# Spreading 1/rms with one-pass matmuls of a diagonal split in two, and another order of the last root

## The chip, the cores and the metric

The kernel runs on one core of a Trainium2 chip. A core has five engines with instruction queues of their own: PE (TensorE, matrix multiply), DVE (VectorE), ACT (ScalarE), POOL (GpSimd) and SP (SyncE, which issues DMAs here). Each works off its queue in order and waits for semaphores of the others. Times are microseconds on the device, from one launch of the whole layer; lower is better. The profile times every instruction of one execution.

## The reference

One decoder layer on x of 512 tokens by 1024 channels, all float32:

```
x = x + 0.5 * rms_norm(swiglu(rms_norm(x, g), w_gu, w_down), g')        # first network, d_ff = 2816
y = hybrid_mixer(rms_norm(x, g))          # RG-LRU channels beside sliding-window attention, then w_o
x = x + rms_norm(y, g')
x = x + 0.5 * rms_norm(swiglu(rms_norm(x, g), w_gu, w_down), g')        # second network
rms_norm(x, g) = x * rsqrt(mean(x * x, over channels) + 1e-6) * g
```

Each norm needs one factor 1/rms for every token. The mixer's recurrent half also has a norm of its own ahead of w_o.

## The kernel before, in words

**Layout.** Nearly everywhere activations lie with channels on the partitions and tokens along the free dimension: eight tiles of 128 channels by 512 tokens. Only the end of the second network has tokens on the partitions, four blocks of 128 tokens.

**Matmuls in three parts.** Weights and activations are split into a high part in the type float32r and a low part, the rest. A product is high x high, high x low and low x high, three matmuls of float32r operands (mm3, L502). The high part of a weight is made on ACT, the low part on DVE or POOL (L194 and L214 lie in these helpers; one weight is shared, half of its low part on DVE and half on POOL, class Shared). An activation's parts are made by x_high (ACT, L580) and x_low (DVE scalar_tensor_tensor, L583).

**From a sum of squares to a factor for each column.** Class InvRms does half of the tokens, 256. stats sums squares over the partitions with small matmuls, so that the sums of two token blocks stand in two columns with tokens on the partitions. invert makes the root on ACT (L556), the reciprocal on DVE (L558), and then a diagonal matrix of the factors on DVE (L560): the identity times the factors, two 128 x 128 blocks side by side, 256 columns. spread multiplies a matrix of ones with it (L564), which puts the factors of all 256 tokens on every partition; its result is read by DVE or copied by ACT. Both operands are float32, and the profile shows two LDWEIGHTS and two MATMUL records for each such matmul.

There are twelve spreads. Pair x is for the first norm (made in InvRmsX.early from sums of squares by token: for each half a sum L1179, the root, the reciprocal, the diagonal). Two single ones scale the first network's output in the first boundary, pair mx is for the mixer's input, pair lru for the recurrent half, two single ones stand in the second boundary, and pair f2 (named nf in the profile) is for the second network's input. A norm's factor is applied after the next products where that can be, so the pairs mx and f2 come in the middle of a stage.

**A boundary** (function boundary) ends one stage and begins the next. The last three output chunks are computed for the first half of the tokens, then for the second, with the first half's statistics and spread put into the second half's matmuls as hooks. Then DVE scales a chunk by the factor (L715), DVE or POOL adds it to the residual (L719), ACT makes its high part (L580) and PE multiplies it (L524, L525); low parts come later (L583 and L531).

**The order** of each engine's queue is the order of the program text. The weights' queue (class Weights) is filled some units ahead at places written by hand (W.fill).

**The end.** For each block of 128 tokens the second network's output is finished in two pieces, the last block in three (512, 256 and 256 columns). For each piece DVE adds the product's bank to a partial sum (L1983), ACT squares it with its sum into one column of the tile ss (L1984), and DVE or POOL multiplies the piece by the gain (L1988). Then DVE adds the columns (for the last block L1986 and L1990), ACT takes the root (L1995), DVE the reciprocal (L1996), and for each piece one instruction that scales and adds x (L1999), after which it is written out.

Of the kernel before, what the change touches and what calls it, by code (L numbers as in the profile page):

```python
# [8 lines left out]
F32 = mybir.dt.float32  # L9
F32R = mybir.dt.float32r  # L10
U8 = mybir.dt.uint8
AF = mybir.ActivationFunctionType
ALU = mybir.AluOpType
AX = mybir.AxisListType

P = 128
T = 512
NB = T // P
D = 1024
# [6 lines left out]
EPS = 1e-6  # L26
# [95 lines left out]
def tile_layer(ctx: ExitStack, tc: tile.TileContext, out: bass.AP, **ins: bass.AP):  # L122
    nc = tc.nc
    pe, dve, act, pool, sync = nc.tensor, nc.vector, nc.scalar, nc.gpsimd, nc.sync

    const = ctx.enter_context(tc.tile_pool(name="const", bufs=1))
# [3 lines left out]
    small = ctx.enter_context(tc.tile_pool(name="small", bufs=4))  # L130
# [6 lines left out]
    HALF = [slice(0, T // 2), slice(T // 2, T)]  # L137
# [6 lines left out]
    def t2k(name, dt=F32):  # L144
        return big.tile([P, T], dt, tag="t2k", name=name, bufs=NT2K)
# [16 lines left out]
    def wt(name, w=T, dt=F32):  # L162
        return tmp.tile([P, w], dt, tag="w", name=name, bufs=NW)
# [23 lines left out]
    class Shared:  # L187


        parts = slice(0, KD // 2), slice(KD // 2, KD)  # L190
# [273 lines left out]
    ident = const.tile([P, P], F32, name="ident")  # L464
# [3 lines left out]
    def filled(name, w, value):  # L468
        t = const.tile([P, w], F32, name=name)
        dve.memset(t, value)  # L470
        return t

    ones = filled("ones", P, 1.0)
    mean_d = filled("mean_d", 1, 1.0 / D)
    mean_c = filled("mean_c", 1, 1.0 / C)
    eps = filled("eps", 1, EPS)
    eps4 = filled("eps4", 1, 4 * EPS)
# [31 lines left out]
    def product(w, xs, sl=ALL, name="", hooks=()):  # L509
        ps = bank(name)  # L510
        hooks = dict(hooks)
        for k, x in enumerate(xs):
            if k in hooks:
                hooks[k]()
            mm3(ps[:, sl], w, k, [t[:, sl] for t in x], k == 0, k == len(xs) - 1)
        return ps
# [22 lines left out]
    class InvRms:  # L539
# [13 lines left out]
        def invert(self, ms, scale=1.0):  # L553
            n = self.name
            rms = small.tile([P, 2], F32, tag="rms", name=f"rms_s{n}")
            act.activation(rms, ms, AF.Sqrt, bias=self.eps, scale=scale)  # L556
            rs = small.tile([P, 2], F32, tag="rs", name=f"rs_{n}")
            dve.reciprocal(rs, rms)  # L558
            self.dg = wt(f"dg_{n}", T)[:, :2 * P].rearrange("p (a b) -> p a b", a=2)
            dve.tensor_tensor(self.dg, ident.unsqueeze(1).to_broadcast([P, 2, P]), rs.unsqueeze(2).to_broadcast([P, 2, P]), op=ALU.mult)  # L560

        def spread(self):
            o = self.ps[:, T // 2:]
            pe.matmul(o, ones, self.dg.rearrange("p a b -> p (a b)"), start=True, stop=True)  # L564
            return o


# [153 lines left out]
    def boundary(res, late, xs, parts, nxt, name):  # L721
# [21 lines left out]
        def spread_a():  # L743
            spread(0)
            steps((0, 1), 0, bcs[0])
# [35 lines left out]
        for k in range(KD):  # L781
            nxt.low(k, 0)
        k_high(ws, banks, nxt.xs, HALF[0], range(4, 6))
        spread(1)
        for k in range(0, KD, 2):
            steps((k, k + 1), 1, bcs[1])
# [571 lines left out]
    parts = [None] * KD  # L1358
    late, h_hbm, decay = [], {}, []
    for g, (f0, f1) in enumerate(GROUPS1):  # L1360
# [18 lines left out]
        for c in range(KD):  # L1379
# [25 lines left out]
            b = pair_banks[c] if c < 2 else product(W.take(), xs, name=f"ya{g}{c}")  # L1405
# [16 lines left out]
    def in_product(name, hooks=(), ahead=AHEAD):  # L1422
        return product(W.take(ahead), mx.xs, name=name, hooks=hooks)
# [79 lines left out]
    for j in range(4):  # L1503
        b = in_product(f"pq{j}")
# [90 lines left out]
    scale = HD ** -0.5  # L1595
# [215 lines left out]
    for c in range(EARLY):  # L1811
# [9 lines left out]
        if c == EARLY - 2:  # L1821
            bcs = [l.spread() for l in lrms]
            for ci in range(KC):
                for h in range(2):
                    dve.tensor_mul(hl[ci][:, HALF[h]], hl[ci][:, HALF[h]], bcs[h])
                y = t2k(f"ylh{ci}", F32R), t2k(f"yll{ci}", F32R)
# [39 lines left out]
    parts = {(tb, dh): hbm.tile([P, T], F32, name=f"yp_b{tb}{dh}") for tb in range(NB) for dh in range(2)}  # L1866
# [29 lines left out]
    def read(half, dh):  # L1896
        for tb in (2 * half, 2 * half + 1):
            in_hbm[tb, dh] = parts[tb, dh]
            parts[tb, dh] = t2k(f"yp{tb}{dh}")
            sync.dma_start(parts[tb, dh], in_hbm[tb, dh])  # L1900
# [3 lines left out]
    def read_x(i):  # L1904
        x = wpool.tile([P, 2 * D], F32, tag="raw", name=f"x_rows{i}", bufs=NRAW)
        for j in range(2):
            x_rows.append(x[:, j * D:(j + 1) * D])
            sync.dma_start(x_rows[-1], x_hbm[(2 * i + j) * P:(2 * i + j + 1) * P])

    grow = []  # L1910

    def read_gain():
        for dh in range(2):
            grow.append(t2k(f"grow{dh}"))
            sync.dma_start(grow[dh], ins["ffn2_post_g"][0:1, dh * T:(dh + 1) * T].to_broadcast([P, T]))

    last = {-1: [lambda: (read(0, 0), read(0, 1), read(1, 0), read(1, 1), read_gain(), read_x(0))],
            2: [lambda: hid.fetched(f0, h_hbm[f0])], 3: [lambda: read_x(1)], 4: [lambda: (hid.split(f0), hid.split(f0 + 1))]}
# [42 lines left out]
    pieces = {tb: [(0, 0, T)] + ([(1, 0, T // 2), (1, T // 2, T)] if tb == NB - 1 else [(1, 0, T)]) for tb in range(NB)}  # L1961

    def place(tb, i):
        dh, c0, c1 = pieces[tb][i]
        return kept[tb // 2, dh][tb % 2][:, c0:c1] if i < 2 else final[:, :c1 - c0]

    def out_products(tb, i, fs):
        dh, c0, c1 = pieces[tb][i]
        for f in fs:
            mm3_out(place(tb, i), hs[f - f0], tb, weights(f, dh), f % 2, slice(c0, c1), i == 2 and f == f0, f == f1 - 1, skip_group_check=True)  # L1970
# [4 lines left out]
    for tb in range(NB):  # L1975
        end = tb == NB - 1
        last = []
        ss = small.tile([P, 3], F32, tag="ss3", name=f"ss_b{tb}")
        tot = small.tile([P, 1], F32, tag="tot", name=f"tot_b{tb}")
        for i, (dh, c0, c1) in enumerate(pieces[tb]):  # L1980
            out_products(tb, i, range(f0 + 2 * ((tb, i) in started), f1))
            y = parts[tb, dh][:, c0:c1]
            dve.scalar_tensor_tensor(y, place(tb, i), -1.0 if dh else 1.0, y, op0=ALU.mult, op1=ALU.subtract if dh else ALU.add)  # L1983
            act.activation(wt(f"ysq{tb}{i}")[:, :c1 - c0], y, AF.Square, accum_out=ss[:, i:i + 1])  # L1984
            if end and i == 2:
                dve.tensor_add(tot, ss[:, 0:1], ss[:, 1:2])  # L1986
            last.append(wt(f"last{tb}{i}")[:, :c1 - c0])
            (dve if end or i else pool).tensor_mul(last[i], y, grow[dh][:, c0:c1])  # L1988
        if end:
            dve.tensor_add(tot, tot, ss[:, 2:3])  # L1990
        else:
            dve.tensor_add(tot, ss[:, 0:1], ss[:, 1:2])

        rs = small.tile([P, 1], F32, tag="rs1", name=f"rs_b{tb}")
        act.activation(rs, tot, AF.Sqrt, bias=eps4, scale=4.0 / D)  # L1995
        dve.reciprocal(rs, rs)  # L1996
        for i, (dh, c0, c1) in enumerate(pieces[tb]):
            y = parts[tb, dh][:, c0:c1]
            dve.scalar_tensor_tensor(y, last[i], rs, x_rows[tb][:, dh * T + c0:dh * T + c1], op0=ALU.mult, op1=ALU.add)  # L1999
            (act if end and i == 1 else sync).dma_start(out[0, tb * P:(tb + 1) * P, dh * T + c0:dh * T + c1], y)  # L2000
# [28 lines left out]
```

## Time and profile before

| what | before |
|---|---|
| median of three runs | 845.54 us (845.32 to 846.01) |
| span of the profiled execution | 843.6 us |
| PE busy | 834.5 us, 99% |
| DVE busy | 732.7 us, 87% |
| ACT busy | 523.8 us, 62% |
| POOL busy | 201.7 us, 24% |
| mean granted TensorE clock | 0.998 |

The span goes from the first to the last instruction of the profiled execution, which has no run time of its own beside it; what lies around it is 1.94 us if it ran like the median. In a row of the time order stand the start in the span, the duration, the engine, the line, the operation, "what is written <- what is read", the shape and the number of instructions that are merged in the row (x8); at the end, in brackets, how long the engine stood idle before it and who ended that. A duration runs from start to complete end, so the next instruction of an engine may start before it. In the chain of waits stand start, length, engine, tile and line.

### The profile page before, as it was taken

The numbers are of one execution on the slowest core, as the hardware profiler recorded it, in microseconds if no ns is written. First come the engines' busy times: TensorE is split into PE (matmuls) and PEld (weight loads), VectorE is DVE, ScalarE is ACT, GpSimd is POOL, SyncE is SP. The second block draws the span as 40 slices with busy tenths as digits, with TensorE's granted clock in tenths as the row PEclk, the third lists the DMA queues.
The fourth block names the chain that finished last, engine by engine and source line by source line (L and its number), as shares of the span: only waits on it lengthen the run. The fifth ranks groups of instructions, "written<-read, shape, count | busy, mean of one in ns | idle before, by whom it ended". The sixth has DMA issues, their size and how long they took to land.

```text
span 843.6 us, 12618 instructions
## 1 busy us (share of the span) xinstructions
PE 834.5 (99%) x4568; PEld 722.6 (86%) x4568; DVE 732.7 (87%) x1020; ACT 523.8 (62%) x874; POOL 201.7 (24%) x214
## 2 busy tenths in 40 slices
PE   9999999999999999999999999999999999999996
PEld 8988888988988998997788899888888888888885
DVE  4978999998979865889899589799998998998996
ACT  6646856666666655456788457436757767666552
POOL 2023000140320333334646055112004113032001
PEclk9999999999999999999999999999999999999999
DMA  7249419397595799222511131169539939769742
GB/s 251 77 131 348 151 59 322 80 254 254 129 248 185 169 261 343 77 79 91 158 50 51 50 110 42 50 137 273 186 108 231 322 91 249 249 154 262 295 137 101
DMA packets 123615, 143.75 MB, mean 170 GB/s; under 512 B 23896, under 2 KB 81568, under 8 KB 123040
## 3 DMA queue, kind: packets, MB, share of 16 engines
q1 hardware_dynamic: 109232, 111.86, 41.6%
q0 software_dynamic: 14176, 30.94, 17.0%
q8 instruction: 36, 0.59, 0.3%
q14 instruction: 27, 0.22, 0.1%
q10 hardware_dynamic: 144, 0.13, 0.0%
HBM read 100.45 MB, written 40.89 MB: 168 GB/s over the span
## 4 chain that ended last, share of the span: by engine, by line
PE 97%; ACT 1%; DVE 1%; DMA 1%; issue 0%; POOL 0%; DVEq 0%; POOLq 0%; ACTq 0%
PE ab L955 10%; PE aa L955 10%; PE da L955 5%; PE db L955 5%; PE yaa L1345 3%; PE bb L955 3%; PE ba L955 3%; PE yda L1345 2%; PE ya L507 2%; PE ya L505 2%; PE ya L506 2%; PE a_first L1205 1%; PE aa L885 1%; PE yab L1875 1%; PE yab L1874 1%; PE yab L1876 1%
## 5 line engine op out<-in xcount | busy, mean ns | idle before, releaser
L1115 POOL DMA_DIRECT2D yp_a<-stage x42 | 36.9, 1085 | 181.2 <-ACT stage L1112 160.9
L1115 POOL DMA_DIRECT2D yp_b<-stage x42 | 36.4, 1091 | 144.6 <-ACT stage L1112 121.1
L505 PE MATMUL ya<-hha,whi_ad 128*128 128x512 f32 x62 | 24.1, 389 | 0.0
L506 PE MATMUL ya<-hla,whi_ad 128*128 128x512 f32 x62 | 24.1, 389 | 0.0
L507 PE MATMUL ya<-hha,wlo_ad 128*128 128x512 f32 x62 | 24.1, 389 | 0.0
L688 POOL TENSOR_TENSOR acca_r<-acca_r,sq_r 128x512 f32<-128x512 f32 x6 | 8.2, 1359 | 51.4 <-ACT sq_r L536 51.4
L1988 POOL TENSOR_TENSOR last<-yp,grow 128x512 f32<-128x512 f32 x3 | 3.9, 1290 | 57.7 <-DVE yp L1983 57.7
L524 PE MATMUL an<-xh_mx,whi_xl 128*128 128x256 f32 x64 | 15.8, 287 | 0.0
L1984 ACT ACTIVATE ysq<-yp 128x512 f32<-128x512 f32 (+1 forms) x9 | 5.3, 585 | 16.5 <-DVE yp L1983 16.0
L525 PE MATMUL an<-xh_mx,wlo_xl 128*128 128x256 f32 x64 | 15.5, 283 | 0.0
L505 PE MATMUL gt<-xh_mx,whi_gt 128*128 128x512 f32 x32 | 14.2, 444 | 0.0
L1112 ACT COPY stage<-yab 128x512 f32<-128x512 f32 x12 | 6.5, 604 | 11.7 <-DMA yp_b<-stage 7.4
L507 PEld LDWEIGHTS ya<-hha,wlo_ad 128*128 128x128 f32 x62 | 11.6, 188 | 2.4
L506 PEld LDWEIGHTS ya<-hla,whi_ad 128*128 128x128 f32 x62 | 11.6, 188 | 2.4
L505 PEld LDWEIGHTS ya<-hha,whi_ad 128*128 128x128 f32 x62 | 11.6, 188 | 2.4
L536 ACT ACTIVATE sq_r<-yp_a 128x256 f32<-128x256 f32 (+1 forms) x10 | 5.0, 502 | 12.9 <-DVE yp_a L678 5.9
L505 PE MATMUL pq<-xh_mx,whi_q 128*128 128x512 f32 x32 | 12.8, 400 | 0.0
L505 PE MATMUL pub<-xh_f,whi_bu 128*128 128x512 f32 x32 | 12.6, 395 | 0.0
L507 PE MATMUL gt<-xh_mx,wlo_gt 128*128 128x512 f32 x32 | 12.6, 394 | 0.0
L505 PE MATMUL pgb<-xh_f,whi_bg 128*128 128x512 f32 x32 | 12.6, 393 | 0.0
L506 PE MATMUL gt<-xl_mx,whi_gt 128*128 128x512 f32 x32 | 12.5, 392 | 0.0
L580 ACT ACTIVATE xh_f<-xT,cols 128x256 fp32r<-128x256 f32 x16 | 8.1, 509 | 7.0 <-DVE xT L719 6.4
(2014 smaller groups left out, 3535.0 us busy)
## 6 DMA issues: line engine op xcount, KB each, us to landing
yp_a<-stage POOLq DMA_DIRECT2D x50, 256.0 KB, 8.9
yp_b<-stage POOLq DMA_DIRECT2D x50, 256.0 KB, 9.2
h_a<-za SPq DMA_DIRECT2D x16, 256.0 KB
hxa<-h_a SPq DMA_DIRECT2D x16, 256.0 KB
h_b<-zb SPq DMA_DIRECT2D x16, 256.0 KB
hxb<-h_b SPq DMA_DIRECT2D x16, 256.0 KB
xn<-in_x SPq DMA_DIRECT2D x8, 256.0 KB
xT_hbm<-xT POOLq DMA_DIRECT2D x2, 1024.0 KB, 9.7
```

Of the source, the lines that this page charges most:

```text
L505: pe.matmul(ps, hi[:, k, :], xh, start=start, stop=False)
L506: pe.matmul(ps, hi[:, k, :], xl, start=False, stop=False)
L507: pe.matmul(ps, lo[:, k, :], xh, start=False, stop=stop)
L524: pe.matmul(ps[:, sl], hi[:, k, :], xh, start=k == 0, stop=False)
L525: pe.matmul(ps[:, sl], lo[:, k, :], xh, start=False, stop=False)
L885: pe.matmul(o, w[:, k, js], x, start=first and i + j + k == 0, stop=k == 3 and i == 2, skip_group_check=True)
L955: pe.matmul(b[tb], x[:, blk], w[:, k, :], start=first and q + k + j == 0, stop=q + k == 2 and j == 2, skip_group_check=True)
L1115: pool.dma_start(o, st.rearrange("p (a b) -> p a b", a=2) if len(o.shape) == 3 else st, accum_op=ALU.add)
L1205: pe.matmul(banks[j][:, HALF[0]], ws[j][part][:, k, :], n1.xs[k][xpart][:, HALF[0]], start=k == 0 and part == xpart, stop=stop and k == KD ...
L1345: pe.matmul(o, a[:, k, ms], x[:, js], start=first and i + k + m % 2 == 0, stop=k == 1 and i == 2, skip_group_check=True)
L1874: pe.matmul(banks[i], hh[:, js], hi[:, k, :], start=first and k == 0, stop=False, skip_group_check=True)
L1875: pe.matmul(banks[i], hh[:, js], lo[:, k, :], start=False, stop=False, skip_group_check=True)
```

## The change

In InvRms the diagonal becomes two: a high part in float32r, written by the same tensor_tensor, and a low part, identity times factor minus the high part, written by two scalar_tensor_tensor of 128 columns, one for each token block. The matrix of ones becomes float32r (by a copy from a float32 one at the start), and spread becomes two matmuls of 256 columns, ones times the high and ones times the low part, summed in the same bank.

At the end, for the last block, the third sum of squares goes to a tile of its own. The other two are summed beside the last Square, already scaled by 4/D and with 4 eps added, and enter the root as its bias, so the root follows the last Square on ACT. The products with the gain of the second and third piece move behind the root in the program; the first stays.

```diff
-    ones = filled("ones", P, 1.0)
+    ones = const.tile([P, P], F32R, name="ones")
+    ones_f = wt("ones_f", P)
+    dve.memset(ones_f, 1.0)
+    dve.tensor_copy(ones, ones_f)
...
             dve.reciprocal(rs, rms)
-            self.dg = wt(f"dg_{n}", T)[:, :2 * P].rearrange("p (a b) -> p a b", a=2)
-            dve.tensor_tensor(self.dg, ident.unsqueeze(1).to_broadcast([P, 2, P]), rs.unsqueeze(2).to_broadcast([P, 2, P]), op=ALU.mult)
+            both = wt(f"dg_{n}", T, F32R)
+            self.dg = [both[:, sl] for sl in HALF]
+            hi, lo = (t.rearrange("p (a b) -> p a b", a=2) for t in self.dg)
+            dve.tensor_tensor(hi, ident.unsqueeze(1).to_broadcast([P, 2, P]), rs.unsqueeze(2).to_broadcast([P, 2, P]), op=ALU.mult)
+            for i in range(2):
+                dve.scalar_tensor_tensor(lo[:, i], ident, rs[:, i:i + 1], hi.bitcast(F32)[:, i], op0=ALU.mult, op1=ALU.subtract)
 
         def spread(self):
             o = self.ps[:, T // 2:]
-            pe.matmul(o, ones, self.dg.rearrange("p a b -> p (a b)"), start=True, stop=True)
+            for i, part in enumerate(self.dg):
+                pe.matmul(o, ones, part, start=i == 0, stop=i == 1)
             return o
...
-            act.activation(wt(f"ysq{tb}{i}")[:, :c1 - c0], y, AF.Square, accum_out=ss[:, i:i + 1])
-            if end and i == 2:
-                dve.tensor_add(tot, ss[:, 0:1], ss[:, 1:2])
+            if i == 2:
+                ss_last = small.tile([P, 1], F32, tag="tot", name="ss_last")
+                act.activation(wt(f"ysq{tb}{i}")[:, :c1 - c0], y, AF.Square, accum_out=ss_last)
+                dve.tensor_scalar(tot, ss[:, 0:1], 4.0 / D, 4 * EPS, op0=ALU.mult, op1=ALU.add)
+                dve.scalar_tensor_tensor(tot, ss[:, 1:2], 4.0 / D, tot, op0=ALU.mult, op1=ALU.add)
+            else:
+                act.activation(wt(f"ysq{tb}{i}")[:, :c1 - c0], y, AF.Square, accum_out=ss[:, i:i + 1])
             last.append(wt(f"last{tb}{i}")[:, :c1 - c0])
-            (dve if end or i else pool).tensor_mul(last[i], y, grow[dh][:, c0:c1])
+            if not end or i == 0:
+                (dve if end or i else pool).tensor_mul(last[i], y, grow[dh][:, c0:c1])
+        rs = small.tile([P, 1], F32, tag="rs1", name=f"rs_b{tb}")
         if end:
-            dve.tensor_add(tot, tot, ss[:, 2:3])
+            act.activation(rs, ss_last, AF.Sqrt, bias=tot, scale=4.0 / D)
+            for i, (dh, c0, c1) in list(enumerate(pieces[tb]))[1:]:
+                dve.tensor_mul(last[i], parts[tb, dh][:, c0:c1], grow[dh][:, c0:c1])
         else:
             dve.tensor_add(tot, ss[:, 0:1], ss[:, 1:2])
-
-        rs = small.tile([P, 1], F32, tag="rs1", name=f"rs_b{tb}")
-        act.activation(rs, tot, AF.Sqrt, bias=eps4, scale=4.0 / D)
+            act.activation(rs, tot, AF.Sqrt, bias=eps4, scale=4.0 / D)
         dve.reciprocal(rs, rs)
```

## The prediction, made before the change was run

> **What bounds the kernel.** I read the page's first part, then who waits for whom on PE, then the time order around each place that the change touches.
>
> ```profile
> span 843.6 us, 12618 instructions
> ...
> PE 834.5 (99%) x4568; PEld 722.6 (86%) x4568; DVE 732.7 (87%) x1020; ACT 523.8 (62%) x874; POOL 201.7 (24%) x214
> ```
>
> ```profile
> PE yeb L1876 <- DVE hls L838: 0.3, 1, 0.3
> ```
>
> PE works 834.5 of 843.6 us, and behind the start its longest wait is 0.3 us. So a microsecond taken off PE is a microsecond off the end, as long as DVE (87% busy) still delivers in time. Where PE is full, DVE has no slack to read from shares; it has to be read at each place.
>
> **Prices.** The chain of waits in time order at the first pair of spreads, a row of PE in time order, DVE rows, and a DVE row that met POOL:
>
> ```profile
> 28.70 0.86 PE rms_x L564 x4
> ```
>
> ```profile
> 354.76 4.00 PE L531 MATMUL an<-xl_mx,whi_xl 128*128 128x256 f32 x32
> ```
>
> ```profile
> 32.89 0.42 DVE L647 TENSOR_TENSOR tb_a<-xb_a,ta_a 128x256 f32<-128x256 f32 x1
> 33.34 0.43 DVE L648 TENSOR_TENSOR tb_a<-xb_a,tb_a 128x256 f32<-128x256 f32 x1
> ```
>
> ```profile
> 351.44 3.25 DVE L583 SCALAR_TENSOR_TENSOR xl_mx<-xT,cols,xh_mx 128x256 fp32r<-128x256 f32 x8
> 354.61 0.48 DVE L715 SCALAR_TENSOR_TENSOR yp_a<-yp_a,half_g,rms_r 128x256 f32<-128x256 f32 x1
> ```
>
> ```profile
> 472.07 0.75 DVE L583 SCALAR_TENSOR_TENSOR yll<-xc,cols,ylh 128x512 fp32r<-128x512 f32 x1 [0.79 <-ACT ylh L580]
> ```
>
> ```profile
> 391.57 1.32 POOL L1473 TENSOR_TENSOR xcl<-xc,xch 128x512 fp32r<-128x512 f32 x1 [1.05 <-ACT xch L1472]
> ```
>
> ```profile
> 391.67 1.77 DVE L1446 SCALAR_TENSOR_TENSOR xc<-xp,cols,xc 128x512 f32<-128x512 f32 x1
> ```
>
> PE: two spreads are four records, 0.86 us, 0.43 a spread. A one-pass matmul of 256 columns is 0.12 (32 of them take 4.00, of which the last alone 0.28), so the two new ones are 0.24: 0.19 saved for each of 12 spreads, 0.38 a pair, 2.28 in all, and that is the most that PE can give. [...]
>
> DVE: the diagonal (256 columns) stays and two scalar_tensor_tensor of 128 columns are added per spread, 24 in all. No row has that size. From above: a whole 256-column one, eight of which start over 351.44 to 354.61, so 0.40 each; from below half of it, 0.20. Between 512 and 256 columns the duration falls from 0.75 to 0.48, so 128 columns fewer are 0.135 less: I take 0.40 - 0.135 = 0.26, the straight line through the nearest rows. The first of the two reads what the diagonal has just written. L648 reads what L647 wrote and starts 0.45 after it, where a 256-column instruction that needs nothing lets the next start after 0.34 (343.00 to 343.34 below): 0.11 more. So DVE is held 0.11 + 2 x 0.26 = 0.63 longer for a spread (bounds 0.40 and 0.90), and the last part is complete 0.45 + 0.26 + 0.34 = 1.05 after the diagonal begins, against 0.43 now.
>
> POOL began 0.10 ahead of the DVE row beside it, which took 1.77 instead of 0.75: it ended at 393.44, 0.55 after POOL's end at 392.89. So a DVE instruction with both inputs in SBUF that comes second stands until POOL is done. [...]
>
> **The change, place by place.** There are six pairs of spreads: x, the boundary after the first network (two single ones), mx, lru, the boundary after the mixer (two single ones), and f2.
>
> *Pair x.*
>
> ```profile
> 21.78 0.29 ACT L556 ACTIVATE rms_sx<-ss_x,eps 128x2 f32<-128x2 f32 x1 [0.83 <-DVE ss_x L1179]
> 21.98 1.19 ACT L580 ACTIVATE xh_a<-xtp,g 128x256 fp32r<-128x256 f32 x3
> ```
>
> ```profile
> 22.70 0.36 PE L524 MATMUL a_first<-xh_a,whi_first 128*128 128x256 f32 x1
> ```
>
> The sum L1179 stands on DVE right behind the first diagonal, ACT's second root has waited 0.83 for it, and the x_high parts stand behind that root. All go 0.63 later. The first x_high takes about 0.4 (1.19 over three) to 0.5, so it is there by 22.5 and PE takes it at 22.70: with 0.1 for the signal 0.15 of slack. PE stands 0.48; the pair itself gives 0.38 later. Net +0.10.
>
> *First boundary.* The first spread comes in the last product before the next stage.
>
> ```profile
> 343.00 0.43 DVE L560 TENSOR_TENSOR dg_r<-ident,rs_r 128x256 f32<-128x256 f32 x1
> 343.34 0.69 DVE L194 TENSOR_TENSOR wlo_xl<-raw_xl__3439,whi_xl 128x512 fp32r<-128x512 f32 x1
> ```
>
> ```profile
> 343.87 1.31 POOL L194 TENSOR_TENSOR wlo_xl<-raw_xl__3439,whi_xl 128x512 fp32r<-128x512 f32 x1 [8.44 <-ACT whi_xl L209]
> ```
>
> ```profile
> 345.52 1.63 ACT L580 ACTIVATE xh_mx<-xT,cols 128x256 fp32r<-128x256 f32 x3 [0.65 <-DVE xT L719]
> ```
>
> ```profile
> 346.22 0.28 PE L524 MATMUL an<-xh_mx,whi_xl 128*128 128x256 f32 x1
> ```
>
> Behind the diagonal DVE does its half of a weight's low part (L194), and POOL the other half from 343.87. With 0.63 more, DVE comes to L194 at 343.97, 0.10 after POOL, the same lead as in the pair at 391.57. It then ends 0.55 after POOL's 345.18, at 345.73, where it ended at 344.03: 1.70 late, and so are the scaling L715, the sum and x_high on ACT. The first x_high ends near 346.05 now and PE uses it at 346.22: slack 0.1. PE stands 1.60; that the spread's own last part comes about 0.2 late lies inside it. The second spread gives 0.19. The eight low parts at 351.44 go later by 1.70 + 0.63 = 2.33 and end at 357.02; PE's matmuls with them go from 354.76 to 356.17 and reach the eighth 7 x 0.12 later, 357.01: even, so 0 to 0.1, taken as 0. Net 1.60 - 0.19 = +1.41.
>
> *Pair mx.*
>
> ```profile
> 373.70 0.17 DVE L558 RECIPROCAL rs_nmx<-rms_snmx 128x2 f32<-128x2 f32 x1 [0.37 <-ACT rms_snmx L556]
> ...
> 374.50 0.43 DVE L560 TENSOR_TENSOR dg_nmx<-ident,rs_nmx 128x256 f32<-128x256 f32 x1
> ```
>
> ```profile
> 376.55 0.38 PE L564 MATMUL rms_nmx<-dg_nmx,ones 128*128 128x256 f32 x1
> ```
>
> DVE arrives 2.33 late from the boundary, less the 0.37 that it idles now ahead of the reciprocal: 1.96. The second diagonal, which ends at 374.93 now, then ends 1.96 + 0.63 later, and the last part 0.62 behind that: 378.14, with the signal 378.24. PE, 1.41 late, begins at 377.96 and asks for the last part three matmuls on, 378.32. It fits, by 0.1 only: -0.38.
>
> *Pair lru.*
>
> ```profile
> 468.25 2.36 DVE L214 TENSOR_TENSOR wlo_wo<-raw_wo__4495,whi_wo 128x1024 fp32r<-128x1024 f32 x2 [0.22 <-ACT whi_wo L209]
> ```
>
> ```profile
> 473.58 0.39 PE L506 MATMUL wo<-yll,whi_wo 128*128 128x512 f32 x1
> ```
>
> 1.26 more on DVE; 0.31 of it fills the hole ahead of L214 (0.22 in the row, and 0.09 by which 256 columns free DVE before they end, 0.43 to 0.34). The rest, 0.95, moves L214, the scaling and the first low part (472.07 to 472.82) to 473.77. With 0.1 for the signal PE takes it at 473.87 instead of 473.58: the 0.38 that the spreads gave is used up, net +0.29.
>
> *Second boundary and pair f2.*
>
> ```profile
> 500.94 0.42 DVE L560 TENSOR_TENSOR dg_r<-ident,rs_r 128x256 f32<-128x256 f32 x1
> 501.98 0.42 DVE L698 COPY y_r<-my 128x256 f32<-128x256 f32 x1 [0.62 <-PE my L507]
> ...
> 503.20 1.20 DVE L719 TENSOR_TENSOR xT<-y_r,xT 128x256 f32<-128x256 f32 x1
> ```
>
> ```profile
> 501.72 2.40 POOL L214 TENSOR_TENSOR wlo_bu<-raw_bu__5190,whi_bu 128x1024 fp32r<-128x1024 f32 x1 [2.46 <-ACT whi_bu L209]
> ```
>
> ```profile
> 505.07 0.31 PE L524 MATMUL mn<-xh_f,whi_bg 128*128 128x256 f32 x1
> ```
>
> ```profile
> 510.40:533.30 22.90, 22.90 (x178) 22.25 (x178) 22.27 (x40) 14.69 (x32) 10.69 (x11) 1.00 0.00 1
> ```
>
> ```profile
> 534.10 0.42 DVE L560 TENSOR_TENSOR dg_nf<-ident,rs_nf 128x256 f32<-128x256 f32 x1
> ```
>
> ```profile
> 535.42 0.38 PE L564 MATMUL rms_nf<-dg_nf,ones 128*128 128x256 f32 x1
> ```
>
> The first spread's two parts fit into the 0.62 that DVE idles before 501.98. The sum L719 ends at 504.40 because POOL holds until 504.12, so PE's 505.07 stays: its 0.19 is lost in front of x_high. The second spread gives 0.19 to PE and 0.63 more work to DVE, which is busy 22.27 of the 22.90 us that follow; what is left I take for gaps between dependent instructions like L647 and L648, which can't be filled. The second diagonal of f2 ends now at 534.52. After: 0.63 from the boundary, 0.63 from the first half's parts and 0.62 from the second's, 536.40; with 0.15 for the signal and weight load PE multiplies at 536.55 and goes on at 536.67. Now it goes on at 535.42 + 0.86 = 536.28. Net for boundary and pair +0.39, said as +0.40.
>
> *Tail.*
>
> ```profile
> 836.39 0.28 PE L1852 MATMUL ybl<-whi_br,hlb 128*128 128x256 f32 x1
> ```
>
> ```profile
> 836.91 0.42 DVE L1983 SCALAR_TENSOR_TENSOR yp<-ybl,yp 128x256 f32<-128x256 f32 x1
> ```
>
> ```profile
> 837.40 0.29 issue
> ```
>
> ```profile
> 838.43 0.29 ACT L1995 ACTIVATE rs_b<-tot_b,eps 128x1 f32<-128x1 f32 x1 [0.23 <-DVE tot_b L1990]
> ```
>
> The last sum y is ready for DVE at 836.70, 0.03 after PE's end at 836.67, but stands behind the product L1988: -0.2. The root no longer waits for L1990: -0.23. The 0.29 of "issue" ahead of the last Square has no cause that I can see; I count half. -0.57, bounds -0.2 and -0.72. The two moved products (0.34 apart) end beside Square and root, and lie on no path. The start-up copy of `ones` has DVE idle and costs nothing.
>
> Sum: 0.10 + 1.41 - 0.38 + 0.29 + 0.40 - 0.57 = **+1.25 us**, span 844.85. The runs' median stands 1.94 above the profiled span (845.54 to 843.6); with the same 1.94 the time is 846.8, 0.15% more. From no change a measurement tells about 0.2%, 1.69 us.
>
> **Rivals.**
> 1. *DVE is first at L194.* For it: it misses by 0.10 only, and with 0.20 per part it would be at 343.85, ahead of POOL. Then the boundary costs 0.63 - 0.1 - 0.19 = 0.34 and the sum is +0.18: 845.7.
> [...]
> 3. *The parts are hidden everywhere*, so PE's 2.28 and the tail's 0.57 come whole: 842.7, faster. It decides if DVE needs under about 0.15 for a spread, since that is the slack at x. Against it: half of a 256-column row is already 0.20.
> 4. *POOL is first at the second boundary too.* The second part there starts at 500.94 + 0.45 + 0.26 = 501.65, 0.07 ahead of POOL's 501.72. If it loses, it stands until 504.12, the spread with it, and PE instead of 502.1 goes on near 504.5: 2.4 more, 849.2, slower. It decides from 0.07 us on.
>
> **How the numbers follow.** Forecast 0.42, rival 1 0.18, rival 2 0.12, rival 3 0.08, rival 4 0.20. The forecast's own range is 846.2 to 848.4: with parts of 0.22 x, lru and f2 cost 0.5 less, with parts of 0.35 they and the low parts of the first boundary 1.3 more, and the tail's bounds add -0.15 and +0.37. A third of it lies above 847.23. Slower: rival 4 and a third of the forecast, 0.34, and a hundredth of rival 1: 0.35. Faster than 843.85: rival 3 and under half of rival 2, 0.13. Same: 0.52. The range 844.0 to 849.3 leaves out rival 3, a third of rival 2 and under half of rival 4, about 0.2.
>
> **What would show it.** On PE four records of 0.12 pitch a pair instead of 0.86. On DVE 24 scalar_tensor_tensor of 128 columns on a line of their own, 0.26 apart. At the first boundary DVE's L194 with over 1.2 us and a PE wait of about 1.6 for x_high; waits of 0.5 at 22.7 and of 0.3 to 0.7 for the low part at 473 and the spread at 535. In the tail the root right behind the last Square. The forecast is wrong if the order of POOL and DVE at 343.9 or 501.7 comes out the other way, or if the parts' price is off by 0.2.

## The result, and the profile after

The changed kernel took 850.91 us (median of five runs, 849.39 to 851.20) where the kernel before took 845.58 on the same chip: a ratio of 1.0058, interval 1.0046 to 1.0070. It is slower by 0.6%. The forecast was 846.8, and the range ended at 849.3. The profiled execution is the run of 849.39, with a span of 847.7: 4.1 us more than the span of 843.6 before. First the page of the changed kernel, then who PE waits for (microseconds in total, how often, the longest):

```profile
span 847.7 us, 12643 instructions
...
PE 834.0 (98%) x4568; PEld 721.1 (85%) x4568; DVE 741.9 (88%) x1045; ACT 523.2 (62%) x874; POOL 201.1 (24%) x214
```

```profile
PE rms_r L572 <- DVE dg_r L567: 2.5, 2, 2.3
...
PE an L527 <- ACT xh_mx L588: 1.1, 1, 1.1
PE a_first L527 <- ACT xh_a L588: 0.6, 1, 0.6
...
PE wo L509 <- DVE yll L591: 0.3, 1, 0.3
PE rms_nf L572 <- DVE dg_nf L565: 0.2, 1, 0.2
```

PE is busy 0.5 us less and stands 4.9 us in these waits, none of which the kernel before had: 2.3 for DVE's second low part (L567) in the first spread of the second boundary, 1.1 and 0.6 for x_high, 0.3 for a low part of lru, 0.2 each for a high and a low part of f2 (the row of the low part is not shown) and 0.2 for the first boundary's spread. The kernel before had no wait of PE over 0.3 behind its start.

Both kernels issue the same instructions in the same order on PE, but for the spreads. So the start of a matmul in the one trace can be set against its start in the other, and the lag shows where time went. Five rows of before that were not shown yet, each behind a pair of spreads, a boundary or a low part (start, duration, engine, line, tiles):

```profile
29.52 0.28 PE L525 MATMUL a_first<-xh_a,wlo_first 128*128 128x256 f32 x1
...
358.60 0.28 PE L524 MATMUL an<-xh_mx,whi_xl 128*128 128x256 f32 x1
...
377.64 0.40 PE L506 MATMUL pv<-xl_mx,whi_kv 128*128 128x512 f32 x1
...
473.80 0.39 PE L507 MATMUL wo<-ylh,wlo_wo 128*128 128x512 f32 x1
...
536.51 0.40 PE L506 MATMUL pub<-xl_f,whi_bu 128*128 128x512 f32 x1
```

and the rows of the changed kernel that answer to these:

```profile
29.90 0.28 PE L528 MATMUL a_first<-xh_a,wlo_first 128*128 128x256 f32 x1
...
360.57 0.28 PE L527 MATMUL an<-xh_mx,whi_xl 128*128 128x256 f32 x1
...
379.21 0.40 PE L509 MATMUL pv<-xl_mx,whi_kv 128*128 128x512 f32 x1
...
475.71 0.40 PE L510 MATMUL wo<-ylh,wlo_wo 128*128 128x512 f32 x1
...
541.28 0.39 PE L509 MATMUL pub<-xl_f,whi_bu 128*128 128x512 f32 x1
```

| stretch | lag at its end, us | it adds | forecast |
|---|---|---|---|
| start and pair x | 29.90 - 29.52 = 0.38 | +0.38 | +0.10 |
| first boundary | 360.57 - 358.60 = 1.97 | +1.59 | +1.41 |
| pair mx | 379.21 - 377.64 = 1.57 | -0.40 | -0.38 |
| pair lru | 475.71 - 473.80 = 1.91 | +0.34 | +0.29 |
| second boundary and pair f2 | 541.28 - 536.51 = 4.77 | +2.86 | +0.40 |
| tail | 847.7 - 843.6 = 4.1 | -0.67 | -0.57 |

Four terms came within 0.2 of the forecast. The first is 0.28 off. One, the second boundary, is 2.46 off, and that is nearly all of the 2.85 between +1.25 and +4.1. What happened there, DVE's rows in order of time, then POOL's row and PE's:

```profile
501.74 0.41 DVE L718 TENSOR_TENSOR accb_r<-accb_r,acca_r 128x256 f32<-128x256 f32 x1
502.60 0.43 DVE L719 TENSOR_TENSOR accb_r<-accb_r,sq_r 128x256 f32<-128x256 f32 x1 [0.46 <-ACT sq_r L539]
...
503.14 0.42 DVE L565 TENSOR_TENSOR dg_r<-ident,rs_r 128x256 fp32r<-128x256 f32 x1
503.60 2.70 DVE L567 SCALAR_TENSOR_TENSOR dg_r<-ident,rs_r,dg_r 128x128 fp32r<-128x128 f32 x2
506.22 0.41 DVE L706 COPY y_r<-my 128x256 f32<-128x256 f32 x1
...
503.68 2.47 POOL L214 TENSOR_TENSOR wlo_bu<-raw_bu__5216,whi_bu 128x1024 fp32r<-128x1024 f32 x1 [2.48 <-ACT whi_bu L209]
...
506.35 0.39 PE L572 MATMUL rms_r<-dg_r,ones 128*128 128x256 f32 x1 [2.28 <-DVE dg_r L567]
```

The two low parts, which take 0.61 together elsewhere, took 2.70. The second of them would have begun at 503.60 + 0.26 = 503.86, and POOL had begun its weight part at 503.68. DVE's row ends 0.15 after POOL's (506.30 and 506.15), and PE stands 2.28 for it. This is the fourth rival of the prediction, to which I gave 0.20.

### The profile page after: what moved, and what is told of

Same layout as the page of the kernel before. It is cut to its first block, busy times and chain, and to the rows that moved or that the text cites. A ratio compares the mean times of both kernels' runs of the same rounds, so it can differ in the third digit from the quotient of the medians.

```text
span 847.7 us, 12643 instructions
## 1 busy us (share of the span) xinstructions
PE 834.0 (98%) x4568; PEld 721.1 (85%) x4568; DVE 741.9 (88%) x1045; ACT 523.2 (62%) x874; POOL 201.1 (24%) x214
## 4 chain that ended last, share of the span: by engine, by line
PE 88%; DVE 6%; ACT 3%; DMA 1%; issue 1%; SPq 1%; DVEq 0%; ACTq 0%
PE ab L963 10%; PE aa L963 10%; PE da L963 5%; PE db L963 5%; PE yaa L1353 3%; PE bb L963 3%; PE ba L963 3%; PE yda L1353 2%; PE ya L508 2%; PE ya L509 2%; PE ya L510 2%; PE aa L893 1%; PE yab L1884 1%; PE yab L1883 1%; PE yab L1882 1%; DVE xl_f L591 1%
## 5 line engine op out<-in xcount | busy, mean ns | idle before, releaser
L527 PEld LDWEIGHTS an<-xh_mx,whi_xl 128*128 128x128 f32 x64 | 12.2, 191 | 1.3 <-ACT xh_mx L588 1.3
L510 PE MATMUL pq<-xh_mx,wlo_q 128*128 128x512 f32 x32 | 12.5, 390 | 0.0
```

The source lines that it names most:

```text
L510: pe.matmul(ps, lo[:, k, :], xh, start=False, stop=stop)
L527: pe.matmul(ps[:, sl], hi[:, k, :], xh, start=k == 0, stop=False)
```

## The experiments

Each run below is set beside runs of the kernel before on the same chip, in three groups whose medians for the kernel before are 845.49, 845.78 and 845.44. The third group (the last run with POOL's weight parts in halves, and the two runs with more DVE instructions) is from another chip; where it is set against the changed kernel's 849.64 of the first group, the two medians of before differ by 0.05. "Whole" is a spread as before: a float32 matmul of the unsplit diagonal, no low parts.

**The changed kernel once more** (no edit).

> The changed kernel as it is, once more. Its five runs went from 849.4 to 851.2, wider than the 0.7 us over which the runs of before lie, and the profiled one, 849.4, is the fastest. Theory 1 (the way in which POOL and DVE meet is the same in every run): the runs stay where they were, the profile shows the second low part of the first spread at the second boundary behind POOL with about 2.7 us for the two, and a PE wait of 2.3. Theory 2 (POOL and DVE meet differently from run to run, since DVE is 0.08 us late for POOL): some run comes out 2.4 us faster, near 847.

849.64 (848.94 to 850.65), 1.0049 with an interval of 1.0035 to 1.0063. In the profile POOL is first again, and here DVE's first low part is the one that stands: it begins at 503.21, 0.04 ahead of POOL's 503.25, and takes 2.54, the two 2.80. So by the starts in a trace a lead of 0.04 was not enough here. There is a PE wait of 2.4. No run came near 847: theory 1. The spread of 1.7 us among its runs stayed unexplained at this point.

**The tail alone.** The kernel before, with the part of the diff that begins at the last Square.

> The kernel before with the change of the tail alone. On PE the changed kernel is 4.77 us behind the kernel before at its last wait, and its span is only 4.1 longer: so the tail gives 0.67, and this run is 845.58 - 0.67 = 844.9. Rival: the tail gives nothing, the 0.67 comes from work that PE's delay had covered: 845.6.

844.83, 0.66 less than before; the interval of the ratio, 0.9982 to 1.0000, ends at no change, so the time alone hardly rules out the rival. The profile does: at PE's last product this run is 0.27 behind the kernel before, and its span is 0.4 to 0.5 shorter, so the tail gives about 0.7 here too.

**The first spread of the second boundary whole.**

```
+WHOLE = ('r20',)      # the names of the spreads that stay as before
...
+if n in WHOLE:
+    self.dg = wt(f"dg_{n}", T)[:, :2 * P].rearrange("p (a b) -> p a b", a=2)
+    dve.tensor_tensor(self.dg, ident..., rs..., op=ALU.mult)
+    return
...
+if self.name in WHOLE:
+    pe.matmul(o, ones.bitcast(F32), self.dg..., start=True, stop=True)
+    return o
```

> [...] Theory 1 (DVE's low part came second to POOL's weight part and stood until POOL ended): 2.4 less than the changed kernel, 847.0 where that has 849.4. Rival (the loss there is the load on DVE, 0.63 us of two more instructions): at most 0.63 less, 848.8 where that has 849.4.

847.32 (1.0021, 1.0013 to 1.0030): 2.3 less than the changed kernel's 849.64 on the same chip, by undoing one spread of twelve. Theory 1; two more instructions on DVE would have been worth 0.63 at most. The wait of 2.3 is gone from the list of PE's waits, the others are still there.

**All four spreads of the boundaries whole.** The same edit with `('r10', 'r11', 'r20', 'r21')`.

> The changed kernel with the four spreads of the two boundaries as before; x, mx, lru, f2 and the tail stay changed. By PE's lag between the two traces x costs 0.38, mx gives 0.40, lru costs 0.34, f2 costs 0.55 and the tail gives 0.67: +0.2, 845.8. If f2 was late only since DVE came late from the boundary (1.26 us of low parts there), f2 gives 0.26 instead and the sum is -0.6: 845.0. Rival (the price lies in the low parts as such, wherever they stand, so that four of twelve spreads take a third of the loss away): 849.1.

845.00 (0.9992, 0.9984 to 1.0001): the 845.0 of the second case. In the profile f2 now gives 0.20 (lag -0.39 behind the second boundary, -0.59 behind f2), where 0.26 was said. The price does not lie in the low parts as such, but in where those of four spreads stand.

**POOL's weight parts in halves.** First all those of the tile `bu`, of which two stand ahead of the second boundary:

```
-low.tensor_sub(two(lo, x), x, two(hi.bitcast(F32), x))
+for ks in shared.parts if name.startswith("bu0_") and low is pool else [slice(0, nk)]:
+    low.tensor_sub(two(lo, x)[:, ks], x[:, ks], two(hi.bitcast(F32), x)[:, ks])
```

> The changed kernel; POOL's weight part at the second boundary (1024 columns, 2.47 us) is issued as two instructions of 512 columns. Theory 1 (DVE's second low part stands until the POOL instruction that began ahead of it has ended): it stands for one of two, about 1.25 us instead of 2.47; PE's wait there falls from 2.3 to about 1.1, and the time by 1.2, to 848.4 where the changed kernel had 849.6. Rival A (POOL's second instruction goes ahead of the waiting DVE one): no difference, 849.6. Rival B (DVE is late there for another reason than POOL): no difference, and the two low parts still take 2.7.

847.73, 1.9 less than the changed kernel's 849.64 (an earlier group), and neither the theory nor the two rivals had that. Its rows:

```profile
502.19 0.43 DVE L720 TENSOR_TENSOR accb_r<-accb_r,sq_r 128x256 f32<-128x256 f32 x1 [0.46 <-DVE accb_r L719]
...
502.81 0.43 DVE L566 TENSOR_TENSOR dg_r<-ident,rs_r 128x256 fp32r<-128x256 f32 x1
503.27 0.61 DVE L568 SCALAR_TENSOR_TENSOR dg_r<-ident,rs_r,dg_r 128x128 fp32r<-128x128 f32 x2
...
503.59 2.70 POOL L215 TENSOR_TENSOR wlo_bu<-raw_bu__5216,whi_bu 128x512 fp32r<-128x512 f32 x2 [2.15 <-ACT whi_bu L209]
```

The second low part begins at 503.27 + 0.26 = 503.53, 0.06 ahead of POOL: DVE is first, both parts take 0.61, and PE does not wait. So the run says nothing on the length of POOL's instruction, and shows the price of the order instead. DVE's diagonal begins 0.33 earlier than in the changed kernel (502.81 against 503.14) and POOL's part 0.09; the edit also halved a POOL instruction at 496 us, and by which way it brought DVE forward is not shown. With only the one instruction in halves that DVE meets:

```
+... if name.startswith("bu0_") and name.endswith("1") and low is pool ...
```

> The changed kernel; of POOL's three weight parts ahead of the second boundary only the last one, which met DVE's low part, is issued as two instructions of 512 columns (in the run with all of them split DVE had come first, so nothing could be seen of the length). Theory 1 (the wait lasts until the POOL instruction that began first has ended): PE's wait falls from 2.3 to about 1.1, the time to 848.4; and with the shorter wait the granted clock stays at 1.00 behind it in all runs, so that they lie within 0.8 of each other. Rival (DVE waits until POOL has no more work): 849.6, spread over 848.9 to 851.2 as before.

```profile
503.71 1.62 DVE L568 SCALAR_TENSOR_TENSOR dg_r<-ident,rs_r,dg_r 128x128 fp32r<-128x128 f32 x2
...
503.79 2.69 POOL L215 TENSOR_TENSOR wlo_bu<-raw_bu__5216,whi_bu 128x512 fp32r<-128x512 f32 x2 [2.48 <-ACT whi_bu L209]
```

```profile
PE rms_r L573 <- DVE dg_r L568: 1.4, 2, 1.2
```

848.71, 0.9 less than 849.64 where 1.2 was expected. Half the columns in a POOL instruction, and the low parts take 1.62 instead of 2.70, 1.08 less, and PE's longest wait is 1.2 instead of 2.3. DVE's row ends at 505.33 and POOL's second instruction at 506.48, so DVE waited here for the instruction that began first, not for POOL's queue. Its runs lie over 1.15 us (848.20 to 849.35), more than the 0.8 that I had expected, though their mean granted clocks are all 0.998 or 0.999. One thing that differs between executions is a wait of PE for ACT near 600 us: 0.5 in this profile and in the repetition's, none in the changed kernel's.

**More DVE instructions ahead.** In the rows of the changed kernel above the sum at 502.60 starts 0.45 after the end of the sum before it (501.74 + 0.41). The same pair of rows in the kernel before stands 0.15 apart:

```profile
499.79 0.41 DVE L710 TENSOR_TENSOR accb_r<-accb_r,acca_r 128x256 f32<-128x256 f32 x1
500.35 0.43 DVE L711 TENSOR_TENSOR accb_r<-accb_r,sq_r 128x256 f32<-128x256 f32 x1 [0.15 <-ACT sq_r L536]
```

Without that 0.30 DVE would have been first. Four or eight short instructions are added where DVE idles at the start:

```
+for _ in range(8):      # or 4
+    dve.memset(ones_f, 1.0)
```

> The changed kernel with eight more short DVE instructions in its first microseconds, where DVE is idle; nothing else is moved. Three profiles in which POOL was first at the second boundary show the last sum of squares ahead of the diagonal starting 0.45 after the sum before it, those without the loss show 0.15. Theory 1 (the extra 0.30 depends on how many DVE instructions stand ahead, since it appears with 17 more and not with 0, 9 or 13): with 25 it can be gone; then DVE is first by about 0.1, PE's 2.3 us wait is gone and the time is 847.2. Rival (the 0.30 comes from the state of the boundary, that is from POOL's and DVE's times there): as the changed kernel, 849.6.

> The same with four more short DVE instructions. Theory 1 (the number of DVE instructions ahead decides): the extra 0.30 is gone or has moved; either 847.2 with DVE first or 849.6 with POOL first, and the profile shows the sum 0.15 or 0.45 after the one before it, in step with that. Rival: 849.6, and 0.45.

With four more:

```profile
501.40 0.41 DVE L720 TENSOR_TENSOR accb_r<-accb_r,acca_r 128x256 f32<-128x256 f32 x1
501.96 0.42 DVE L721 TENSOR_TENSOR accb_r<-accb_r,sq_r 128x256 f32<-128x256 f32 x1 [0.15 <-ACT sq_r L541]
...
503.02 0.61 DVE L569 SCALAR_TENSOR_TENSOR dg_r<-ident,rs_r,dg_r 128x128 fp32r<-128x128 f32 x2
...
503.34 2.55 POOL L214 TENSOR_TENSOR wlo_bu<-raw_bu__5220,whi_bu 128x1024 fp32r<-128x1024 f32 x1 [2.48 <-ACT whi_bu L209]
```

The sum starts 0.15 after the end of the one before it, the second low part at 503.28 is 0.06 ahead of POOL's 503.34, and the time is 847.49 (1.0022, 1.0014 to 1.0031): 2.1 less than the changed kernel, for four instructions that do nothing. With eight more the rows are the same there (second part 503.35, POOL 503.42), and the median is 848.14, 0.9 above the expected 847.2, with runs from 846.72 to 850.03. The profiled one is among the longest, by another cause: near 588 us PE waits 1.5 for ACT, which has waited 4.65 for a weight's transfer, 1.1 longer than in the changed kernel, and near 601 us it waits 0.7 for ACT again. The repetition of the changed kernel waited as long for that transfer (4.79), but its PE was 1.7 later there and met no wait; so in this run most of what was saved at the second boundary was lost again to that transfer. That the number of DVE instructions ahead decides the 0.30 is shown (0.45 with 17 more than in the kernel before, 0.15 with 21 and with 25); why it does is not.

**POOL's half at the first boundary in halves.**

```
 dk, pk = self.parts
 dve.tensor_sub(lo[:, dk], x[:, dk], hi[:, dk])
+m = (pk.start + pk.stop) // 2
+for ks in (slice(pk.start, m), slice(m, pk.stop)):
+    pool.tensor_sub(lo[:, ks], x[:, ks], hi[:, ks])
```

> The changed kernel; POOL's half of the weight's low part at the first boundary (512 columns, 1.33 us) is issued as two instructions of 256 columns. Theory 1 (DVE's own half comes second and stands until POOL's instruction ends): POOL's first instruction ends about 0.65 earlier, so DVE's half takes 1.1 instead of 1.77, PE's wait for x_high falls from 1.1 to about 0.5, and the time from 849.6 to 849.0. Rival (PE's wait there is the 0.63 that the low parts take on DVE and the length of POOL's instruction does not matter): 849.6.

849.87, no less than 849.64. But the place itself did what theory 1 says:

```profile
343.94 1.22 DVE L194 TENSOR_TENSOR wlo_xl<-raw_xl__3447,whi_xl 128x512 fp32r<-128x512 f32 x1
...
343.82 1.94 POOL L197 TENSOR_TENSOR wlo_xl<-raw_xl__3447,whi_xl 128x256 fp32r<-128x256 f32 x2 [8.45 <-ACT whi_xl L212]
```

```profile
PE an L530 <- ACT xh_mx L591: 0.6, 1, 0.6
```

DVE's half takes 1.22 instead of 1.77, and PE's wait for x_high is 0.6 instead of 1.1. The 0.5 gained there was lost again at the second boundary of the profiled run, where PE waited 2.29 as in the changed kernel, and then ran slower. Its spread in order of time, and the windows behind it (PE's, PEld's, DVE's, ACT's and POOL's busy time with the count of instructions, then the granted clock):

```profile
502.78 0.34 PE L575 MATMUL rms_r<-dg_r,ones 128*128 128x256 f32 x1
505.40 0.47 PE L575 MATMUL rms_r<-dg_r,ones 128*128 128x256 f32 x1 [2.29 <-DVE dg_r L570]
505.67 0.42 PE L511 MATMUL my<-ylh,whi_wo 128*128 128x256 f32 x1
505.88 0.42 PE L512 MATMUL my<-yll,whi_wo 128*128 128x256 f32 x1
```

```profile
506.00:508.80 2.80, 2.80 (x15) 2.80 (x15) 2.57 (x7) 1.72 (x4) 1.67 (x2) 0.50 0.83 267
509.50:512.00 2.50, 2.50 (x23) 2.50 (x22) 1.66 (x5) 0.82 (x2) 0.00 (x0) 1.00 0.09 24
```

From 505.67 to 508.87 the 256-column matmuls follow each other at 0.21 instead of 0.12; the granted clock of the 2.8 us in the window is 0.50. Against the kernel before the lag grows by 1.3 us on this stretch. The profiles of the changed kernel and of its repetition have 1.00 behind the same wait.

For the runs without a profile there is only each run's mean granted clock, from which 3.2 us at 0.50 would take 0.002. In this kernel it is 0.998 and 0.999 for the two shortest runs and 0.997 for the other three; in the changed kernel 0.999 for the two shortest and 0.997, 0.997 and 0.995 for the three from 850.91 to 851.20. In the repetition 850.45 has 0.997, but 850.65 has 0.999, and the kernel before has runs of ordinary length at 0.997. So a drop in some runs and not in others, worth 1.3 us each time, fits most of the spread of the changed kernel's runs (1.8 and 1.7 us), but not every run, and it is not shown for each of them.

**High parts only.** The low parts and the second matmul are left out, so the factors are rounded to float32r.

```
-for i in range(2):
-    dve.scalar_tensor_tensor(lo[:, i], ident, rs[:, i:i + 1], hi.bitcast(F32)[:, i], ...)
-for i, part in enumerate(self.dg):
-    pe.matmul(o, ones, part, start=i == 0, stop=i == 1)
+pe.matmul(o, ones, self.dg[0], start=True, stop=True)
```

> The changed kernel without the low parts: the spreads are one one-pass matmul of the rounded diagonal, and DVE has nothing more to do than in the kernel before. This leaves out the low part of the factors. Theory 1 (PE's saving is whole where DVE is not later, and the price is all DVE's low parts): each spread saves 0.43 - 0.12 = 0.31 on PE; the four single ones ahead of x_high or low parts lose part of it to waits that PE then meets (x_high had 0.1 of slack), so between 6 x 0.31 and 12 x 0.31 plus the tail's 0.66: 842.9 to 841.1, best guess 842.0. Rival (one-pass spreads bring PE nothing at the end, whatever DVE does): 844.8, the tail alone.

842.21 (0.9959, 0.9945 to 0.9972), where 842.0 was the guess. PE's saving arrives at the end when DVE has nothing more to do. Against its own runs of before it is 3.57 faster, where the changed kernel in its repetition is 4.15 slower: the low parts, with the matmuls that read them, cost 7.7 us, and 2.3 of that is the wait at the second boundary.

**Two clean pairs and the tail.** x and mx in two parts, the other eight spreads whole; at x the sum of the second half goes ahead of the first half's low parts:

```
 dve.tensor_add(ss, sx[:, :, 0], sx[:, :, 1])
+if self.half:
+    n1.rms[0].low_part()
 self.invert(ss, 1.0 / D)
+if self.half:
+    self.low_part()
```

> Only two of the six pairs are spread in two parts, x and mx, and the tail is changed; at x the sum of the second half is put ahead of the first half's low parts, so that ACT's second root and x_high are not late. Theory 1 (a pair whose low parts lie beside other work gives 0.38): 845.5 - 0.38 - 0.38 - 0.66 = 844.1. Rival (the 1.26 of DVE work per pair comes back later, where DVE is full): mx gives nothing in the end, 844.4 to 844.8.

844.07 (0.9983, 0.9975 to 0.9992): the predicted time, and faster than both kernels. The rival's 844.4 lies inside the interval, so the profile has to decide: PE does not wait at x, at mx or at any spread, its lag falls by 0.39 over pair x (-0.34 to -0.73) and by 0.40 over mx (-0.72 to -1.12), and behind f2 it is still -1.17. So mx keeps its gain.

## Why the prediction was wrong, point by point

*The step that failed* is the sentence on the second boundary, "The first spread's two parts fit into the 0.62 that DVE idles before 501.98". I had them begin 0.07 ahead of POOL. With the 1.96 by which PE was late there that is 503.61 against POOL's 503.68, and POOL did begin at 503.68. DVE's second part came at 503.86: the sum ahead of the diagonal started 0.30 later behind its predecessor than before, and 0.25 of it reached the part. Nothing in the trace of before announces that 0.30, but the margin of 0.07 was known, and a miss there was known to cost 2.4. Where the 0.30 is away, in the run with four more instructions, the second part is 0.06 ahead where 0.07 was forecast, and the time is 847.49, inside the range. A forecast that rests on 0.07 us, with parts whose price I knew to 0.2, deserves about even chances against its rival, not 0.42 to 0.20. As a mechanism rival 4 was right in place (2.28 of PE wait), in price (847.7 + 1.7 = 849.4 where it said 849.2) and in its deciding point: 0.06 or 0.07 ahead there was no such wait, in three profiles, and 0.18 behind it was whole, 2.28. The repetition shows it whole for a part that began 0.04 ahead, so of the 0.07 of the forecast only some 0.02 was margin. Rival 4 named the event and its price, though, and not its cause: that DVE would be 0.25 late was not in it.

*The range* ended 0.1 above rival 4's own time and left room for nothing else there. The profiled run lies on its edge and the median 1.6 above. What lies above fits a clock that dropped behind such a wait, as to 0.50 behind the 2.29 in the run with POOL's half in halves (the three runs from 850.91 on have the low mean clocks, 0.995 to 0.997), which no row of before could show, since PE had no such wait there; for these runs it is not shown.

*Prices of the parts.* At the first boundary, in the changed kernel:

```profile
343.39 0.42 DVE L565 TENSOR_TENSOR dg_r<-ident,rs_r 128x256 fp32r<-128x256 f32 x1
343.85 0.61 DVE L567 SCALAR_TENSOR_TENSOR dg_r<-ident,rs_r,dg_r 128x128 fp32r<-128x128 f32 x2
344.38 1.77 DVE L194 TENSOR_TENSOR wlo_xl<-raw_xl__3447,whi_xl 128x512 fp32r<-128x512 f32 x1
...
344.26 1.33 POOL L194 TENSOR_TENSOR wlo_xl<-raw_xl__3447,whi_xl 128x512 fp32r<-128x512 f32 x1 [8.45 <-ACT whi_xl L209]
```

The next instruction begins 344.38 - 343.39 = 0.99 after the diagonal, where 0.34 + 0.63 = 0.97 was forecast; the last part is complete at 344.46, 1.07 after it, forecast 1.05. The straight line between 512 and 256 columns held down to 128. The 0.1 that the forecast gives a signal was an estimate without a row behind it. In the changed kernel PE begins 0.05 to 0.06 after the end of the DVE row that it waited for (506.30 to 506.35 at the second boundary, 475.32 to 475.38 at lru, 540.77 to 540.83 at f2's low part); at f2's high part, where 0.15 stood for signal and weight load, it is 0.15 (540.12 to 540.27).

*First boundary.* DVE's L194 came 0.12 after POOL's (forecast 0.10), took the same 1.77 as the pair of rows it was priced from, and x_high came late as said. At x_high (346.22 before, 348.19 now) the lag had risen by 1.59, forecast 1.60. Of the 0.19 that the second spread gives nothing was left by 360.57: 0.1 was lost at once, since the matmul behind the wait is followed by the next only after 0.23 (348.19 to 348.42) and not 0.12, and 0.1 at the low parts, which I had called even.

*Pair x.* The sum of the second half stands 0.99 behind the first diagonal instead of 0.35, the 0.63 of the forecast. The rest of the 0.38 is the start, which differs between executions:

```profile
19.35 1.28 ACT L556 ACT_TABLE_LOAD   x1
```

```profile
19.69 1.28 ACT L559 ACT_TABLE_LOAD   x1
```

ACT is 0.34 late before the first changed instruction has run on it. In the repetition it is 0.07 early (19.28) and the lag behind the pair is -0.01. So the pair itself costs about 0.05, forecast 0.10.

*mx, lru.* Right within 0.05 each, with the low part of lru 0.3 late as said.

*Pair f2.* In the run with four more instructions, where the 2.3 is away, second boundary and f2 together still add 0.68 (lag 1.56 behind lru, 2.24 behind f2) against +0.40: two waits of 0.2 for f2's parts, and 0.2 for the boundary's own. The span of that profile is 1.6 above the kernel before, where the forecast's case had 1.25, and these 0.28 are the larger part of the difference. The median of its runs is 2.05 above; the profiled run is the shortest of them, and the rest is not accounted for.

*Tail.* The pieces, from the last Square on:

```profile
837.70 0.42 ACT L1984 ACTIVATE ysq<-yp 128x256 f32<-128x256 f32 x1 [0.56 <-DVE tot_b L1986]
...
838.43 0.29 ACT L1995 ACTIVATE rs_b<-tot_b,eps 128x1 f32<-128x1 f32 x1 [0.23 <-DVE tot_b L1990]
```

```profile
841.95 0.42 ACT L1994 ACTIVATE ysq<-yp 128x256 f32<-128x256 f32 x1
...
842.49 0.29 ACT L2004 ACTIVATE rs_b<-ss_last,tot_b 128x1 f32<-128x1 f32 x1
```

PE's last product begins 4.78 later than before (841.17 against 836.39), y comes 4.58 later, the last Square 4.25, the root 4.06. So y gave 0.20 as forecast, the hop 0.19 for 0.23, and the "issue" of 0.29, of which I had counted half for want of a cause, went whole (4.58 - 4.25 = 0.33). The row of before puts the Square's wait of 0.56 down to DVE's sum of the other columns (L1986), but that sum stands behind the Square in the program, so the Square can't have waited for it. From the start of y to the Square it is 0.79 in the kernel before and 0.45 or 0.46 in all twelve profiles with the new tail, so the tail's edit took the 0.33 away. The only thing that it changes at the Square is the tile into which its sum goes, which it shared before with the Square ahead of it; that the shared tile made the wait is likely, and no run shows it alone.

## What to carry to other kernels

Where one engine's instruction stands until another engine's ends, as DVE's low part stood here behind POOL's weight part (2.70 us for the two parts instead of 0.61), and the forecast has one of them first by less than its own uncertainty, write both cases with equal weight; the cost of losing was what was left of the other's instruction, here 2.3 us (503.86 to 506.15) for an instruction of 0.26. Split such a spread only where nobody waits soon for what stands behind it on DVE: mx gave 0.40 as it was and x 0.39 once its second sum stood ahead of the low parts; in the changed kernel the five pairs other than mx lost all of their 0.38 and more. A releaser that a profile names is worth checking against the order of the program: what stands later in it can't have been waited for.

## What the runs showed of the hardware that I had not expected

The granted clock fell to 0.50 behind a PE idle time of 2.29 us, in one of three profiles with such a wait: the window from 506.00 to 508.80 has 0.50, and the matmuls follow each other at 0.21 instead of 0.12 for 3.2 us (505.67 to 508.87); the rows are above. Why it fell there and stayed at 1.00 behind the other two waits is not shown.

That a DVE instruction with both inputs in SBUF stood until the POOL instruction beside it ended was shown by 2.70, 1.62 and 0.61 us for the same two low parts, behind 1024 columns, behind 512, and first. In the kernel before, beside POOL's part from 501.72 to 504.12, the copy out of PSUM (501.98) took 0.42 and the sum with both inputs in SBUF (503.20) 1.20, where the same two took 0.41 each when POOL idled at their start (506.32 and 505.10).

The start of a DVE sum moved by 0.30 us with the number of DVE instructions ahead of it: 0.45 to 0.47 behind the end of its predecessor with 17 more than before (six profiles), 0.15 with 0, 1, 9, 13, 21 and 25 more (seven). What it waits for is open.
